# One Conformer-RWKV block on one core: PSUM evacuations ahead in their queues, a copy from ACT to POOL, an output product begun early, smaller modulation loads

## The chip, the cores and the metric

The program runs on one core of a Trainium2 chip, as one launch. The metric is the device time of an execution in microseconds; the kernel before was timed three times.

## The reference

One layer on 512 positions of 1024 features, in float32. The parts that the change touches, shortened:

```python
mod = silu(c) @ w_ada + b_ada            # six rows of 1024: shift1, scale1, gate1, shift2, scale2, gate2
u = modulate(rms_norm(x), shift1, scale1) @ w_in      # conv, RWKV and gate columns
y_conv = silu(layer_norm(depthwise_conv(za * sigmoid(zb), 31 taps))) @ w_conv_pw
# RWKV, 16 heads of 64: r, k, v, decay w, a, g from u and its shift by one position
S = S * w + (S @ (-kk)) * (kk * a) + v * k            # one step per position
y = S @ r
y_rwkv = ((group_norm(y) + bonus) * g) @ w_o
merged = sigmoid(g_conv) * y_conv + sigmoid(g_rwkv) * y_rwkv
x = x + gate1 * (merged @ w_out)
h2 = modulate(rms_norm(x), shift2, scale2)
return rms_norm(x + gate2 * (relu(h2 @ w_ff1) ** 2 @ w_ff2))
```

## The kernel before, in words

Features lie on partitions, the 512 positions along the row. A product with a weight matrix is made in blocks of 128 output columns. For each block `wload` (L218 to L225) brings 512 KB of weights (raw), ACT casts them to a high part wH (L223) and POOL subtracts it from them for a low part wL (L224). The block then takes 24 matmuls, for each of eight row blocks wH on the high and on the low part of the data, then wL on the high part; `wmul` issues them at L231 to L233, `block` at L528. Two raw, two wH and two wL buffers are there, three PSUM banks for sums.

The RWKV recurrence is solved in chunks of 64 positions, eight chunks, for four groups of four heads (two blocks of 128 features, b = 0 and 1). A group goes through these steps:
- keys (L691 to L694 on POOL) and `decay_k` (L700 to L707) prepare the key tile BK. Its third part is a copy of 64 partitions by 512 elements of its first part, made by ACT at L704; POOL makes k times kp at L705.
- `transposed` (L729), `gram` (L741) and `products` form the products within the chunks.
- `group_solve` inverts the triangular parts on DVE with 31 steps (L795 to L807) while TensorE has other work; `group_solve2` follows with the small products sW (L824) and sX (L831).
- `group_chain` walks the chunks. Each link is, on TensorE, L846 and L848 (ch), L859 (ch from F) and L874 (ch from UV), with the state S on DVE at L881. Between them ACT copies F (L852) and one half of UV (L862), DVE the other half (L863). In the chain of group g the keys of group g+1 are prepared as well (`between`).
- `group_post` normalizes Y on DVE (L905 to L914), then per block transposes it (post, L927), scales it with vb (L928), multiplies by g (L931) and adds (L932).

TensorE's order is pinned there. So that it has work during the solve and the chains, the blocks of w_in still to come (k, r, v, conv and gate columns) stand in a queue, and `fill(n)` issues their next n matmuls. SOLVED says how many fills stand in a solve, STAGE = 4 how many at each place in a chain. When a block ends, its sum leaves PSUM: through `shifted` (ACT L271, DVE L272) for k, r and v, through a sigmoid for a conv gate (L552) or a gate column (L947), through a product on DVE (L557) for the conv input.

The 31 convolution taps are DVE's (L155, drawn one at a time by `tap`), with five taps made by ACT into nsq (two buffers, L572) that POOL adds (L573); L575 joins them, L578 adds to csum. A scheduler orders the instructions on each engine by its own estimate of the times and by priorities; `tc.high_priority(offset=URGENT)` moves an instruction ahead, as it does F, UV and S in the chain. Each engine then runs its queue strictly in order. SP issues all the DMA.

After RWKV follow the product with w_o (the layer norm of the convolution lies inside it), with w_pw, with w_out, and the feed-forward part. The modulation rows come from w_ada: `ada_sum(m, half, pieces, alloc)` loads a half row of 2 MB in pieces and sums them on DVE (L141, L143). In the late stages a piece is 1 MB and there are three buffers (adaw); row 4's second half and row 3's first are loaded in the product with w_pw, row 3's second in that with w_out.

The functions that the change touches:

Of the kernel before, what the change touches and what calls it, by code (L numbers as in the profile page):

```python
# [28 lines left out]
SOLVED, LAST = 148, 20  # L29
# [28 lines left out]
def tile_block(ctx: ExitStack, tc: tile.TileContext, xT, vec, cst, x0, w_ada, w_in, w2a2, g2w,  # L58
# [459 lines left out]

    def pin(i):
        return tc.keep_in_program_order(i)  # L520
# [26 lines left out]
    def conv_in(p):  # L547
        sz = []

        def gate(acc):  # L550
            sz.append(t2k(tag="cv", bufs=2))
            act.activation(sz[0], acc, AF.Sigmoid)  # L552

        def times(acc):
            z = mid.tile([P, PAD + T], F32, name=nm("z"), tag="z", bufs=3)
            pool.memset(z[:, 0:PAD], 0.0)
            dve.tensor_tensor(z[:, PAD:], acc, sz[0], ALU.mult)  # L557
            set_z(p, z)

        return [((p, "b"), block(D + p * P, gate)), ((p, "z"), block(p * P, times))]  # L560
# [57 lines left out]
    def k_block(G, b):  # L618
        def done(acc):
            p = G.blocks[b]  # L620
            G.k[b] = t2k(tag="kk", bufs=2)
            shifted(acc, G.k[b], 8 + p)
            G.sq[b] = t2k()
            act.activation(G.sq[b], G.k[b], AF.Square, scale=V("k_k", p))

        return ("k", G.blocks[b]), block(R0 + D + G.blocks[b] * P, done)

    def r_block(G, b):
        def done(acc):
            G.r[b] = t2k()  # L630
            shifted(acc, G.r[b], G.blocks[b])

        return ("r", G.blocks[b]), block(R0 + G.blocks[b] * P, done)

    def v_block(G, b):
        def done(acc):
            G.v[b] = t2k()
            shifted(acc, G.v[b], 16 + G.blocks[b])

        return ("v", G.blocks[b]), block(R0 + 2 * D + G.blocks[b] * P, done)  # L640

    def low_rank(G, b):
# [17 lines left out]
        dve.tensor_tensor_scan(G.sg[b], cmask, pw, 0.0, ALU.mult, ALU.add)  # L660
# [24 lines left out]
    def keys(G, b):  # L685

        p, k, a = G.blocks[b], G.k[b], G.a[b]
        kP, kp = G.Pi[b], t2k()
        G.ap[b], G.kp[b] = kP, kp
        BK = G.BK[b] = atile("BK", (P, NCH, 3 * C), 2)  # L690
        pool.tensor_tensor(kP, k, G.Pi[b], ALU.mult)  # L691
        act.activation(kp, a, AF.Identity, scale=V("k_a", p), bias=ka1[:, p:p + 1])
        pool.tensor_tensor(BK[:, :, 0:C], r3(kP), r3(kp), ALU.mult)
        pool.tensor_tensor(kP, kP, a, ALU.mult)  # L694

    def decay_k(G, b):
        p, k, a = G.blocks[b], G.k[b], G.a[b]
        prn = pmisc(name="prn")
        for q in range(4):
            pin(pe.matmul(prn[:, q * P:(q + 1) * P], e4[:, q, :], G.rn[:, b, :], start=True, stop=True))  # L700
        ap = G.ap[b]
        BK = G.BK[b]
        dve.scalar_tensor_tensor(BK[:, :, C:2 * C], r3(ap), V("k_k", p), r3(prn), ALU.mult, ALU.mult)
        act.copy(BK[64:128, :, 2 * C:3 * C], BK[64:128, :, 0:C])  # L704
        pool.tensor_tensor(G.kp[b], k, G.kp[b], ALU.mult)  # L705
        kkn = G.kkn[b] = t2k()
        dve.scalar_tensor_tensor(kkn, k, V("k_k", p), prn, ALU.mult, ALU.mult)  # L707
# [38 lines left out]
    def values(G, b):  # L746
# [6 lines left out]
        with tc.high_priority(offset=URGENT):  # L753
# [6 lines left out]
        dve.tensor_tensor(v, pb, v, ALU.mult)  # L760
        nc.sync.dma_start(vb_d[p], v)

    def products(G):
# [4 lines left out]
        for b in range(NB):  # L768
# [3 lines left out]
            for e in range(2):  # L772
                for cq in range(2):
                    gram(G, b, e, cq)
                    tap()
                    fill(STAGE)

# [58 lines left out]
    def group_chain(G, between):  # L836
# [4 lines left out]
        for c in range(NCH):  # L841
# [9 lines left out]
            with tc.high_priority(offset=URGENT):  # L851
                act.copy(Fs, pf)  # L852
# [8 lines left out]
            with tc.high_priority(offset=URGENT):  # L861
# [3 lines left out]
            if c < NCH - 1 and S is not None:  # L865
                sp = atile("sp", (P, NB, C))
                with tc.high_priority(offset=URGENT):
                    for b in range(NB):
                        act.activation(sp[:, b], S[:, b], AF.Copy, scale=G.PC[:, b, c:c + 1])
            if c < NCH - 1:  # L870
# [5 lines left out]
                with tc.high_priority(offset=URGENT):  # L876
# [23 lines left out]
    def group_post(g, G, Y):  # L900
# [19 lines left out]
        for b in range(NB):  # L920
# [7 lines left out]
            dve.scalar_tensor_tensor(o, pt, V("gn_g", p), o, ALU.mult, ALU.add)  # L928
# [3 lines left out]
            dve.scalar_tensor_tensor(o, o, V("gn_b", p), pg, ALU.add, ALU.mult)  # L932
# [62 lines left out]
    fill(14)  # L995
# [6 lines left out]
    for g in range(4):  # L1002
# [12 lines left out]
        if g < 3:  # L1015
# [3 lines left out]
            fill(max(SOLVED - 14 - used[0], 6))  # L1019
            low_rank(Gn, 1)  # L1020
            fill(14)
        else:
            fill(SOLVED - LAST - used[0])
        fill(4)
        group_solve2(G)
        if g == 3:
# [12 lines left out]
    fill(36)  # L1039
    next(post, 0)  # L1040
    while queue:
        fill(1)
    tap(200)
# [6 lines left out]
    for j in range(KC):  # L1050
        if j < 6:
            t = t2k()
            nc.sync.dma_start(t, yo_d[j])
        else:
            t = G.vb[j - 6]
        act.copy(yH(j), t)
        dve.tensor_tensor(yL(j), t, yH(j), ALU.subtract)
    adac = lambda n: cpool.tile([P, n, 512], F32, name=nm("adac"), tag="adac", bufs=2)
    cH, cL = pair(), pair()
    ct8 = []  # L1060
    for j in range(KC):
        gt = t2k(tag="cv", bufs=2)
        nc.sync.dma_start(gt, gate_d[8 + j])
        acc = dense(w_o, 0, j * P, yH, yL)
# [44 lines left out]
    adan = lambda n: pools["B"].tile([P, n, 512], F32, name=nm("adaw"), tag="adaw", bufs=3)  # L1109
# [3 lines left out]
    for j in range(KC):  # L1113
# [6 lines left out]
        if j == 1:  # L1120
            sums.append(ada_sum(4, 1, (4, 4), adan))
# [4 lines left out]
        if j == 4:  # L1126
            sums = [ada_sum(3, 0, (4, 4), adan)]
# [5 lines left out]
    for j in range(KC):  # L1133
# [5 lines left out]
        if j == 1:  # L1139
            sums.append(ada_sum(3, 1, (4, 4), adan))  # L1140
        if j == 3:
# [45 lines left out]
    for g in range(4):  # L1187
        if g:
            rH, rL = pair(g8), pair(g8)
        for f in range(0 if g else EARLY, 8):  # L1190
            relu2(f, dense(w_ff1, 0, (g * 8 + f) * P, h2H, h2L))
            if g == 0 and f in (3, 4):
                sums = sums + [ada_sum(5, f - 3, (4, 4), adan)] if f == 4 else [ada_sum(5, 0, (4, 4), adan)]
# [114 lines left out]
```

## Time and profile before

| what | us |
|---|---|
| three runs: median (lowest to highest) | 1146.67 (1142.85 to 1154.36) |
| profiled execution | 1142.26 |
| its span | 1140.2 |

An engine is busy while an instruction of it runs. PE is TensorE, PEld its weight loads, DVE VectorE, POOL GpSimd, ACT ScalarE, SP the engine that issues DMA. The granted clock (PEclk) is a share of full speed, 2.4 GHz. In a timeline a row names its start, its length, engine, line, operation and tiles; the bracket holds the idle time of the engine just before it, and which instruction ended that. Buffer numbers are left out there. "x64" is a count of equal instructions that follow each other. Some small matmuls appear as two records, so that a set of four is x8.

### The profile page before, as it was taken

What the parts mean: (1) busy time and instruction counts of PE and PEld (TensorE: products, weight loads), DVE (VectorE), ACT (ScalarE), POOL (GpSimd) and SP (SyncE); (2) the same over time, 40 slices, a digit from 0 to 9 for tenths busy, and PEclk for the clock granted to TensorE, in tenths of its full rate; (3) what the DMA queues carried; (4) which work ended last, traced back from release to release, by engine and by line L of the source; (5) the groups of instructions that cost most, each with busy time, mean ns of one, the idle gap of its engine ahead of it and who ended that gap; (6) DMA issues with size and microseconds to landing.
All of it is one profiled execution on the core that took longest, in us unless ns stands there. A gap on an engine that the chain in (4) does not pass through costs nothing. (4 is left out here: it accounts for less than half of the span.)

```text
span 1140.2 us, 16153 instructions
## 1 busy us (share of the span) xinstructions
PE 1059.0 (93%) x6290; PEld 833.9 (73%) x6290; DVE 735.7 (65%) x1128; ACT 504.0 (44%) x856; POOL 498.7 (44%) x290
## 2 busy tenths in 40 slices
PE   6897999999879999999899988998999999999997
PEld 5775777777657766777666766886888888888886
DVE  5876587688747786698869566878513513522545
ACT  5557455655454746445443442345312413322431
POOL 4746343644271634426234343452444444444441
PEclk9999899999989998999899988999999999999998
DMA  9721232214211231117425889842333333333332
GB/s 322 220 65 51 61 116 62 84 61 133 63 47 59 63 119 34 57 51 238 138 75 175 272 288 335 282 124 72 95 92 93 94 94 107 94 93 93 102 100 75
DMA packets 188923, 136.74 MB, mean 120 GB/s; under 512 B 5424, under 2 KB 162480, under 8 KB 188848
## 3 DMA queue, kind: packets, MB, share of 16 engines
q1 hardware_dynamic: 188848, 135.73, 38.5%
q8 instruction: 49, 0.80, 0.3%
q14 instruction: 26, 0.21, 0.1%
HBM read 121.55 MB, written 14.16 MB: 119 GB/s over the span
## 5 line engine op out<-in xcount | busy, mean ns | idle before, releaser
L224 POOL TENSOR_TENSOR wL<-raw,wH 128x1024 fp32r<-128x1024 f32 x142 | 342.9, 2415 | 501.6 <-ACT wH L223 486.8
L528 PE MATMUL mm<-b,wH 128*128 128x512 f32 x832 | 283.2, 411 | 1.5 <-ACT wH L223 1.5
L223 ACT CAST wH<-raw 128x1024 fp32r<-128x1024 f32 x142 | 148.8, 1049 | 305.5 <-PE mm L232 204.5
L528 PEld LDWEIGHTS mm<-b,wH 128*128 128x128 f32 x832 | 156.9, 193 | 37.2 <-ACT wH L223 2.0
L528 PE MATMUL mm<-b,wL 128*128 128x512 f32 x416 | 171.8, 413 | 4.5 <-POOL wL L224 4.5
L155 DVE SCALAR_TENSOR_TENSOR acc<-z,vt,acc 128x512 f32<-128x512 f32 x192 | 143.6, 748 | 2.2
L232 PE MATMUL mm<-g,wH 128*128 128x512 f32 x328 | 128.2, 391 | 1.1 <-DVE g L1161 0.9
L231 PE MATMUL mm<-g,wH 128*128 128x512 f32 x328 | 128.5, 392 | 0.0
L233 PE MATMUL mm<-g,wL 128*128 128x512 f32 x328 | 127.8, 390 | 0.0
L231 PE MATMUL mm<-b,wH 128*128 128x512 f32 x304 | 121.2, 399 | 4.7 <-ACT wH L223 4.7
L233 PE MATMUL mm<-b,wL 128*128 128x512 f32 x304 | 120.6, 397 | 3.1 <-POOL wL L224 3.1
L232 PE MATMUL mm<-b,wH 128*128 128x512 f32 x304 | 120.2, 396 | 1.7 <-DVE b L1169 1.7
L1159 DVE TENSOR_TENSOR t2k<-t2k 128x512 f32<-128x512 f32 x32 | 72.7, 2278 | 57.5 <-ACT t2k L1156 57.2
L528 PEld LDWEIGHTS mm<-b,wL 128*128 128x128 f32 x416 | 80.6, 194 | 23.2 <-POOL wL L224 5.5
L1203 DVE SCALAR_TENSOR_TENSOR x<-mm,cols,x 128x512 f32<-128x512 f32 x31 | 23.3, 751 | 114.4 <-PE mm L233 114.4
L232 PEld LDWEIGHTS mm<-g,wH 128*128 128x128 f32 x328 | 61.6, 188 | 15.3 <-DVE g L1161 2.2
L231 PEld LDWEIGHTS mm<-g,wH 128*128 128x128 f32 x328 | 61.6, 188 | 14.1 <-ACT g L1160 1.2
L231 PEld LDWEIGHTS mm<-b,wH 128*128 128x128 f32 x304 | 58.4, 192 | 17.9 <-ACT wH L223 5.6
L233 PEld LDWEIGHTS mm<-g,wL 128*128 128x128 f32 x328 | 61.6, 188 | 12.9 <-issue 0.2
L233 PEld LDWEIGHTS mm<-b,wL 128*128 128x128 f32 x304 | 58.3, 192 | 16.2 <-POOL wL L224 4.3
L232 PEld LDWEIGHTS mm<-b,wH 128*128 128x128 f32 x304 | 58.4, 192 | 14.5 <-DVE b L1169 2.1
L1160 ACT CAST g<-t2k 128x512 fp32r<-128x512 f32 x32 | 19.8, 621 | 72.4 <-DVE t2k L1159 72.4
(305 smaller groups left out, 1737.7 us busy)
## 6 DMA issues: line engine op xcount, KB each, us to landing
raw<-in_w_ff_dram SPq DMA_DIRECT2D x64, 512.0 KB, 4.0
raw<-in_w_in_dram SPq DMA_DIRECT2D x54, 512.0 KB, 3.8
adaw<-in_w_ada_dram SPq DMA_DIRECT2D x10, 1024.0 KB, 7.3
gate<-cv SPq DMA_DIRECT2D x24, 256.0 KB, 3.1
adac<-in_w_ada_dram SPq DMA_DIRECT2D x24, 256.0 KB, 4.0
wa<-in_w_ada_dram SPq DMA_DIRECT2D x11, 512.0 KB, 5.4
raw<-in_w_o_dram SPq DMA_DIRECT2D x8, 512.0 KB, 4.2
t2k<-gate SPq DMA_DIRECT2D x16, 256.0 KB, 4.9
```

What stands on the lines that cost most here:

```text
L155: dve.scalar_tensor_tensor(dst if i == n - 1 else so_far, row, col, so_far, ALU.mult, ALU.add)
L223: act.copy(wH, raw)
L224: last_low[0] = pool.tensor_tensor(wL, raw, wH, ALU.subtract)
L231: steps.append(pe.matmul(acc, wH[:, kc, :], aH(kc), start=kc == 0, stop=False))
L232: steps.append(pe.matmul(acc, wH[:, kc, :], aL(kc), start=False, stop=False))
L233: steps.append(pe.matmul(acc, wL[:, kc, :], aH(kc), start=False, stop=kc == KC - 1))
L528: pin(pe.matmul(acc, a_[:, kc, :], b_(kc), start=kc == n == 0, stop=end))
L1159: dve.tensor_tensor(t, t, t, ALU.mult)
L1160: act.copy(rH(f), t)
L1203: dve.scalar_tensor_tensor(x1(j), acc, ada[:, 40 + j:41 + j], x1(j), ALU.mult, ALU.add)
```

## The change

- `lead()`: the instructions that take a finished sum out of PSUM (sigmoids, `shifted`, conv products, the decay scan of `low_rank`, the bonus product, the two operations of `group_post`) get the priority that F and UV have.
- The copy in BK is POOL's, directly after the product that it copies, in `keys`; k times kp is moved from `decay_k` to the end of a block's products (it stays on POOL).
- SOLVED is a tuple, one count per group: 138, 150, 146 and 140 instead of 148 three times and 128. `fill(22)` stands for `fill(14)` before the first `decay_k`, and `fill(STAGE)` is added after each `group_solve2`.
- After the last chain, `fill(36)` (of which the queue held 26 matmuls) goes. The first two blocks of w_o are begun on row blocks 0 to 5 (36 pinned matmuls) before the last `group_post`, and finished on row blocks 6 and 7 after it (12).
- The late modulation rows come in pieces of 0.5 MB into six buffers, and row 3 is loaded wholly in the product with w_out, at j = 0 and 2, its column made at j = 5.

Lines of the changed kernel are other numbers: L703, L704, L705 and L787 are the POOL operations L693, the new copy, L694 and L705 of before; L578, L579, L581 and L584 are L572, L573, L575 and L578; L863, L873, L880, L885, L907 are L852, L862, L869, L874, L896; L938, L940, L943 and L945 are L927, L928, L931 and L932; L1080 is the begun w_o product; L1064 is L1056.

```diff
-SOLVED, LAST = 148, 20
+SOLVED = (138, 150, 146, 140)
...
+    def lead():
+        return tc.high_priority(offset=URGENT)
...
             sz.append(t2k(tag="cv", bufs=2))
-            act.activation(sz[0], acc, AF.Sigmoid)
+            with lead():
+                act.activation(sz[0], acc, AF.Sigmoid)
...
-            shifted(acc, G.r[b], G.blocks[b])
+            with lead():
+                shifted(acc, G.r[b], G.blocks[b])
...
-        dve.tensor_tensor_scan(G.sg[b], cmask, pw, 0.0, ALU.mult, ALU.add)
+        with lead():
+            dve.tensor_tensor_scan(G.sg[b], cmask, pw, 0.0, ALU.mult, ALU.add)
...
         pool.tensor_tensor(BK[:, :, 0:C], r3(kP), r3(kp), ALU.mult)
+        pool.tensor_copy(BK[64:128, :, 2 * C:3 * C], BK[64:128, :, 0:C])
         pool.tensor_tensor(kP, kP, a, ALU.mult)
...
-        act.copy(BK[64:128, :, 2 * C:3 * C], BK[64:128, :, 0:C])
-        pool.tensor_tensor(G.kp[b], k, G.kp[b], ALU.mult)
...
                     tap()
                     fill(STAGE)
+            pool.tensor_tensor(G.kp[b], G.k[b], G.kp[b], ALU.mult)
...
-            dve.scalar_tensor_tensor(o, pt, V("gn_g", p), o, ALU.mult, ALU.add)
+            with lead():
+                dve.scalar_tensor_tensor(o, pt, V("gn_g", p), o, ALU.mult, ALU.add)
...
-            dve.scalar_tensor_tensor(o, o, V("gn_b", p), pg, ALU.add, ALU.mult)
+            with lead():
+                dve.scalar_tensor_tensor(o, o, V("gn_b", p), pg, ALU.add, ALU.mult)
...
-    fill(14)
+    fill(22)
     decay_k(G, 0)
...
-            fill(max(SOLVED - 14 - used[0], 6))
+            fill(max(SOLVED[g] - 14 - used[0], 6))
...
-            fill(SOLVED - LAST - used[0])
+            fill(SOLVED[g] - used[0])
         fill(4)
         group_solve2(G)
+        fill(STAGE)
...
     next(post)
-    fill(36)
-    next(post, 0)
     while queue:
         fill(1)
-    tap(200)
...
+    for j in range(6):
+        t = t2k()
+        nc.sync.dma_start(t, yo_d[j])
+        split_rows(j, t)
+    begun = []
+    for j in range(2):
+        wH, wL, raw = wload(w_o, 0, j * P)
+        acc = psum("mm", 3)
+
+        def some(kcs, wH=wH, wL=wL, acc=acc):
+            steps = []
+            for kc in kcs:
+                for n, (a_, b_) in enumerate(((wH, yH), (wH, yL), (wL, yH))):
+                    steps.append(pin(pe.matmul(acc, a_[:, kc, :], b_(kc), start=kc == n == 0, stop=kc == KC - 1 and n == 2)))
+            return acc, steps
+
+        some(range(6))
+        begun.append(some)
+    next(post, 0)
+    for j in (6, 7):
+        split_rows(j, G.vb[j - 6])
+    tap(200)
+
+    def out_product(j):
+        if j > 1:
+            return dense(w_o, 0, j * P, yH, yL)
+        acc, steps = begun[j]((6, 7))
...
-    adan = lambda n: pools["B"].tile([P, n, 512], F32, name=nm("adaw"), tag="adaw", bufs=3)
+    adan = lambda n: pools["B"].tile([P, n, 512], F32, name=nm("adaw"), tag="adaw", bufs=6)
...
-            sums.append(ada_sum(4, 1, (4, 4), adan))
+            sums.append(ada_sum(4, 1, (2,) * 4, adan))
...
-        if j == 4:
-            sums = [ada_sum(3, 0, (4, 4), adan)]
...
-        if j == 1:
-            sums.append(ada_sum(3, 1, (4, 4), adan))
-        if j == 3:
+        if j in (0, 2):
+            sums = ([] if j == 0 else sums) + [ada_sum(3, j // 2, (2,) * 4, adan)]
+        if j == 5:
             with after_dense():
                 ada_col(3, sums)
```

The order on POOL in the first group's chain, where the second group's keys are prepared; before:

```order
L573 TENSOR_TENSOR co_1637<-co_1637,nsq_1821 128x512
L693 TENSOR_TENSOR BK_1721<-t2k_1658,t2k_1720 128x8x64
L694 TENSOR_TENSOR t2k_1658<-t2k_1658,t2k_1302 128x512
L224 TENSOR_TENSOR wL_1745<-raw_1742,wH_1744 128x1024
L705 TENSOR_TENSOR t2k_1720<-kk_1082,t2k_1720 128x512
L693 TENSOR_TENSOR BK_1838<-t2k_1664,t2k_1837 128x8x64
L694 TENSOR_TENSOR t2k_1664<-t2k_1664,t2k_1456 128x512
L705 TENSOR_TENSOR t2k_1837<-kk_1248,t2k_1837 128x512
L573 TENSOR_TENSOR co_1637<-co_1637,nsq_1891 128x512
```

and now:

```order
L579 TENSOR_TENSOR co_1639<-co_1639,nsq_1824 128x512
L703 TENSOR_TENSOR BK_1723<-t2k_1660,t2k_1722 128x8x64
L704 COPY BK_1723<-BK_1723 64x8x64
L705 TENSOR_TENSOR t2k_1660<-t2k_1660,t2k_1310 128x512
L224 TENSOR_TENSOR wL_1746<-raw_1743,wH_1745 128x1024
L703 TENSOR_TENSOR BK_1841<-t2k_1666,t2k_1840 128x8x64
L787 TENSOR_TENSOR t2k_1722<-kk_1064,t2k_1722 128x512
L704 COPY BK_1841<-BK_1841 64x8x64
L705 TENSOR_TENSOR t2k_1666<-t2k_1666,t2k_1454 128x512
L787 TENSOR_TENSOR t2k_1840<-kk_1248,t2k_1840 128x512
L579 TENSOR_TENSOR co_1639<-co_1639,nsq_1893 128x512
```

The names are the tiles of this chain: wL_1745 and wL_1746 are the same weights, nsq_1891 and nsq_1893 the same tap. Each BK product is followed by its copy, one k-times-kp product has moved behind the wL and one before the second copy, and the same tap comes behind one copy more after the wL.

ACT writes those taps into the two nsq buffers. In the same chain, from the fourth UV copy to the fifth; before:

```order
L862 COPY UV_1223<-ch_1789 64x2x64
L223 CAST wH_1923<-raw_1921 128x1024
L704 COPY BK_1838<-BK_1838 64x8x64
L892 COPY Yt_1569<-Y_1762 128x256
L869 ACTIVATE sp_1868<-S_1808,PC_819 128x64 x2
L896 COPY Sd_630<-S_1808 64x2x64
L852 COPY F_1835<-ch_1826 128x128
L896 COPY Sd_630<-S_1808 64x2x64
L572 ACTIVATE nsq_2011<-z_455,vt 128x512
L572 ACTIVATE nsq_2206<-z_1349,vt 128x512
L862 COPY UV_1223<-ch_1857 64x2x64
```

and now, from F before the fourth:

```order
L907 COPY Sd_629<-S_1762 64x2x64 x2
L863 COPY F_1786<-ch_1777 128x128
L578 ACTIVATE nsq_2011<-z_455,vt 128x512
L578 ACTIVATE nsq_2207<-z_1349,vt 128x512
L873 COPY UV_1231<-ch_1792 64x2x64
L903 COPY Yt_1571<-Y_1765 128x256
L880 ACTIVATE sp_1870<-S_1811,PC_819 128x64 x2
L907 COPY Sd_630<-S_1811 64x2x64
L863 COPY F_1838<-ch_1829 128x128
L907 COPY Sd_630<-S_1811 64x2x64
L873 COPY UV_1231<-ch_1859 64x2x64
```

The two taps that stood between the fourth and the fifth UV copy stand ahead of the fourth; nsq_2207 takes the buffer of nsq_1893.

The order on ACT around the fourth UV copy of the second group's chain; before:

```order
L896 COPY Sd_629<-S_2924 64x2x64
L852 COPY F_2958<-ch_2949 128x128
L896 COPY Sd_629<-S_2924 64x2x64
L704 COPY BK_2896<-BK_2896 64x8x64
L704 COPY BK_3020<-BK_3020 64x8x64
L862 COPY UV_2388<-ch_2964 64x2x64
```

and now:

```order
L880 ACTIVATE sp_2994<-S_2943,PC_1657 128x64 x2
L863 COPY F_2977<-ch_2968 128x128
L907 COPY Sd_629<-S_2943 64x2x64 x2
L578 ACTIVATE nsq_3198<-z_1592,vt 128x512
L873 COPY UV_2388<-ch_2983 64x2x64
L578 ACTIVATE nsq_3239<-z_1592,vt 128x512
```

Both copies L704 are gone from the place ahead of UV; a tap into nsq stands there instead, which before came behind it.

The order on TensorE after the last chain, around the two transposes of `group_post`; before:

```order
L231 MATMUL mm_5676<-c_5571,wH_5672 128x512
L927 MATMUL post_5545<-ct,Yt_5043 128x128 x4
L931 MATMUL g_5551<-sgx,t2k_5500 128x512
L232 MATMUL mm_5676<-c_5573,wH_5672 128x512
L927 MATMUL post_5556<-ct,Yt_5043 128x128 x4
L233 MATMUL mm_5676<-c_5571,wL_5673 128x512
L231 MATMUL mm_5676<-c_5571,wH_5672 128x512
L232 MATMUL mm_5676<-c_5573,wH_5672 128x512
L233 MATMUL mm_5676<-c_5571,wL_5673 128x512
L931 MATMUL g_5562<-sgx,t2k_5502 128x512
L231 MATMUL mm_5615<-c_5572,wH_5611 128x512
```

and now:

```order
L1080 MATMUL mm_5605<-c_5549,wH_5601 128x512
L1080 MATMUL mm_5605<-c_5547,wL_5602 128x512
L938 MATMUL post_5626<-ct,Yt_5086 128x128 x4
L943 MATMUL g_5632<-sgx,t2k_5539 128x512
L938 MATMUL post_5637<-ct,Yt_5086 128x128 x4
L943 MATMUL g_5643<-sgx,t2k_5541 128x512
L1080 MATMUL mm_5580<-c_5547,wH_5576 128x512
L1080 MATMUL mm_5580<-c_5549,wH_5576 128x512
L1080 MATMUL mm_5580<-c_5547,wL_5577 128x512
```

Before, matmuls of w_o stood between the transposes and the gate products. Now the four follow each other, behind the 36 begun matmuls, and mm_5580 on the high and low parts of rows 6 and 7 comes after them.

## Rows read from the trace of the kernel before

**Rows 1.** Page, part 1: busy us (share of the span) xinstructions; PEld loads weights.

```profile
PE 1059.0 (93%) x6290; PEld 833.9 (73%) x6290; DVE 735.7 (65%) x1128; ACT 504.0 (44%) x856; POOL 498.7 (44%) x290
```

**Rows 2.** Windows: stretch, length, busy (x) by engine, PEclk, DMA share, GB/s.

```profile
329.00:339.20 10.20, 5.80 (x46) 5.47 (x47) 3.12 (x7) 4.76 (x11) 10.04 (x7) 0.50 0.27 79
547.40:554.20 6.80, 6.51 (x78) 5.06 (x80) 5.57 (x8) 2.19 (x4) 0.00 (x0) 0.51 0.01 3
697.60:707.80 10.20, 7.12 (x16) 5.19 (x17) 4.52 (x8) 2.61 (x3) 4.72 (x2) 0.51 1.06 333
```

**Rows 3.** Timeline, PE: start us, us, operation, xcount [idle before <-releaser].

```profile
115.75 0.79 PE L528 MATMUL mm<-b,wL 128*128 128x512 f32 x1 [3.11 <-POOL wL L224]
...
204.83 0.45 PE L874 MATMUL ch<-UV,bkT 128*64 128x64 f32 x8 [0.29 <-DVE UV L863]
...
207.26 0.50 PE L528 MATMUL mm<-b,wL 128*128 128x512 f32 x1 [0.42 <-POOL wL L224]
...
333.40 0.70 PE L874 MATMUL ch<-UV,bkT 128*64 128x64 f32 x8 [6.67 <-DVE UV L863]
...
405.28 0.50 PE L655 MATMUL pa<-XA,w2H 128*128 128x512 f32 x1 [2.29 <-DVE vb L932]
...
433.44 0.22 PE L831 MATMUL sX<-TT,s 32*32 32x32 f32 x2 [1.49 <-DVE t2k L660]
...
464.85 0.45 PE L874 MATMUL ch<-UV,bkT 128*64 128x64 f32 x8 [2.27 <-DVE UV L863]
...
547.69 1.92 PE L824 MATMUL sW<-s,G 32*32 32x32 f32 x64 [3.61 <-DVE s L805]
...
585.48 0.70 PE L874 MATMUL ch<-UV,bkT 128*64 128x64 f32 x8 [1.04 <-DVE UV L863]
...
609.78 0.66 PE L927 MATMUL post<-ct,Yt 128*128 128x128 f32 x4 [0.76 <-DVE Yt L914]
...
699.47 0.79 PE L231 MATMUL mm<-b,wH 128*128 128x512 f32 x1 [2.78 <-ACT wH L223]
...
701.90 0.80 PE L233 MATMUL mm<-b,wL 128*128 128x512 f32 x1 [1.22 <-POOL wL L224]
```

**Rows 4.** Chain of work that ended last, in order of time: start, us.

```profile
622.84 0.23 PE mm L231
```

**Rows 5.** Timeline, POOL: columns as in rows 3.

```profile
0.87 0.53 POOL L118 MEMSET cmask<- 128x512 f32 x1
...
113.35 2.34 POOL L224 TENSOR_TENSOR wL<-raw,wH 128x1024 fp32r<-128x1024 f32 x1
...
204.85 2.36 POOL L224 TENSOR_TENSOR wL<-raw,wH 128x1024 fp32r<-128x1024 f32 x1
...
212.23 1.29 POOL L573 TENSOR_TENSOR co<-co,nsq 128x512 f32<-128x512 f32 x1
...
328.52 2.35 POOL L224 TENSOR_TENSOR wL<-raw,wH 128x1024 fp32r<-128x1024 f32 x1
...
459.63 1.29 POOL L573 TENSOR_TENSOR co<-co,nsq 128x512 f32<-128x512 f32 x1 [2.56 <-ACT co L568]
```

**Rows 6.** Timeline, ACT, in the second and third chain.

```profile
314.50 1.28 ACT L682 ACT_TABLE_LOAD   x1
...
332.13 0.61 ACT L704 COPY BK<-BK 64x512 f32<-64x512 f32 x1 [6.83 <-POOL BK L693]
...
463.47 0.72 ACT L572 ACTIVATE nsq<-z,vt 128x512 f32<-128x512 f32 x1 [1.79 <-POOL co L573]
```

**Rows 7.** Page, part 5: group xcount | busy us, mean ns | idle before.

```profile
L155 DVE SCALAR_TENSOR_TENSOR acc<-z,vt,acc 128x512 f32<-128x512 f32 x192 | 143.6, 748 | 2.2
```

**Rows 8.** Timeline, DVE, after the last chain.

```profile
597.50 1.22 DVE L905 TENSOR_REDUCE st<-Yt 128x16 f32<-128x1024 f32 x1 [1.32 <-ACT Yt L892]
...
608.50 1.22 DVE L914 TENSOR_TENSOR Yt<-Yt,st 128x1024 f32<-128x1024 f32 x1
```

**Rows 9.** Timeline, SP, its DMA queue, in the product with w_pw.

```profile
679.43 9.69 SPq L166 DMA_DIRECT2D adaw<-in_w_ada_dram  x2
```

## What the change is predicted to do

> **What bounds the kernel now.** I read four views in this order. The page: TensorE is busy 1059.0 of the 1140.2 us span [rows 1], so it is the bound, and only what happens in its 81 us of idle time can move the total. The windows by stretch: after a wait of some length TensorE's granted clock stands at 0.50 or 0.51 of full, which is the 1.2 GHz level, for some us more; 5.80, 6.51 and 7.12 us of busy time lie in three such stretches, so each of them loses 2.9 to 3.5 us beyond the wait itself [rows 2]. TensorE's timeline: the waits that end on another engine [rows 3]. Then the timelines of POOL, ACT, DVE and SP around these places, and the order of the changed kernel beside them. In a chain (L846 to L896) TensorE runs in program order and alternates short products with fills of four matmuls at 0.23 us each [rows 4]; ACT and POOL run in order too, so a wait of ACT for POOL stops the chain's copy behind it.
>
> **The sum, part by part.** All times are of the profiled execution, 1142.26 us (span and 2.06 around it); it lies 0.4% under the median of 1146.67 and 0.05% under the fastest run. TensorE's work hardly changes, so I count its waits and its clock.
>
> A copy of 64x512 on POOL shows nowhere. Below stands a memset of 128x512 at 0.53, above a two-input operation at 1.29 [rows 5]. I take 0.9, the middle, since it reads one operand where the one has none and the other two. The Trainium skill ("GPSIMD Engine Reference", section "Engine selection") says that one-input operations run near line rate there and two-input ones at about half of VectorE's speed. No row here shows the copy; by that rule it would be near the memset's 0.53 (an estimate), and the sum below about 2 us smaller.
>
> *Start of the RWKV stage, +1.1 (0 to 2).* TensorE waits 3.11 at 115.75 for the wL that POOL makes from 113.35 [rows 3, 5]. The two copies go onto POOL before this wL and one L787 moves behind it: 1.8 less 1.25 later, 0.55; the first transposes, 0.6 of work that stood in this gap, now come behind it. The 8 added fills hide an earlier small wait, but only bring TensorE to this wL sooner.
>
> *First solve, +0.3 (0 to 2).* Ten fills fewer, 2.3, against 8 more before it; VectorE's own stalls there shrink too.
>
> *First chain, +6.6, and +3 for the clock.* Here the change costs. Before, POOL's wL (204.85 + 2.36) came with a wait of only 0.42 at 207.26 [rows 3, 5], since its first reader stood behind a link of the chain. By the order the new weight block begins two fills sooner, so its first wL matmul stands ahead of the set of L874 that ran at 204.83. TensorE reaches it at about 204.0; POOL has a copy more in front and ends at 207.2 + 0.9 = 208.1: idle 4.1. Then the next UV copy on ACT stands behind an nsq (L578) that needs the buffer which POOL's L579 frees. After the wL POOL has five two-input operations (a step is 1.25, [rows 5]: 1.29 less overlap) and a copy: 208.1 + 6.25 + 0.9 = 215.25; nsq, UV and VectorE's half add 1.2: 216.5. Without that, TensorE would be at this L885 at 208.1 + 0.5 (two fills) + 0.35 (a set) + 2.0 (204.83 to 207.26 less 0.42) + 2.3 (eight fills and a set) = 213.3: idle 3.2. Together 7.3, less the 0.42 and 0.29 there were. Two new waits of this size cost the clock 0 to 3.5 each [rows 2]; I take 1.5 each.
>
> *Second chain, -3.0 (0 to -9.5).* This is the place that the moved copy is about: ACT's L704 waited 6.83 for POOL, L862 and VectorE's L863 behind it, and TensorE waited 6.67 at 333.40, then ran at half clock [rows 2, 3, 6]. With L704 gone from ACT, its queue has another waiter at the same place: nsq_3198 stands directly ahead of UV, and needs POOL's L579 for nsq_2965. Before wL_2929 POOL now has three operations fewer and a copy more (3 x 1.25 - 0.9 = 2.85), and one table load of 1.28 less on ACT ahead of its inputs [rows 6]: wL ends at 328.52 + 2.35 - 2.85 - 1.28 = 326.7. TensorE needs it in the third link's first fills, near 323, and waits some 3.6. L584 and L579 end at 329.2, nsq, UV and L874 at 330.4, against 333.40. Half clock follows these waits as it did that one.
>
> *Third group, -3.5 and +5.1.* The waits at 405.28 (2.29, for VectorE's vb) and 433.44 (1.49, for L660) go, as both operations now lead VectorE's queue: with a little left over, -3.5 (0 to -5). In its chain TensorE waited 2.27 at 464.85, since ACT's nsq waited for POOL to 463.47 [rows 3, 6]. The order keeps both nsq before this UV. POOL gets two copies (1.8) and a second wL (2.36) ahead of the L573 in question, and starts up to two table loads later (2.0); its idle 2.56 at 459.63 [rows 5] takes some: 1.8 + 2.36 + 2.0 - 2.56 = +3.6 (0 to 4.5). For the clock +1.5.
>
> *Fourth group, -6.5.* The wait of 3.61 at 547.69 meets 12 more fills (2.8) and one VectorE operation of 0.75 [rows 7] less in its solve: -3.5, and of the 3.2 for the clock 2 come back. At 585.48 the cast and the sigmoid ahead of UV are gone: -1.0.
>
> *End of RWKV, +7.0, and +2 for the clock.* VectorE's normalization runs from 597.50 to 608.50 + 1.22 = 609.7 [rows 8]. Before, 26 fills and 25 w_o matmuls (11.7 us) covered it, and the transposes waited 0.76 [rows 3]. The 26 fills are now spent earlier (8 + 16 + 2), so 36 w_o matmuls, 8.3, stand there: 0.76 + 15 x 0.23 = 4.2, and 0.6 more since ACT casts a weight ahead of the last Y copy: 4.8, or +4.0. Then post, g, post, g stand without a filler between them, and 12 w_o matmuls wait for rows 6 and 7: two L155, L940, L141, L945 on VectorE (5 x 0.66), POOL's two additions for csum that ACT now takes first, two casts. This takes about 9.3, TensorE's work in it 4.4: idle 4.9, against some 2 before: +3.0.
>
> *w_pw, -6.5 (0 to -7.5).* SP stood 9.69 at the fourth 1 MB piece, waiting for one of three buffers, with weights behind it [rows 9]; TensorE waited 2.78 and 1.22 [rows 3] and lost 3.5 to the clock. The pieces for row 3 leave this stage: 4.0 and 2.5 of the 3.5.
>
> *w_out, +1 (0 to 4).* Eight half-size pieces enter here, four of which wait for VectorE to free buffers, with weights queued behind them on SP; the worst is what w_pw had, 4.0.
>
> The half pieces elsewhere and the remaining leads cost nothing: they lie beside a TensorE that doesn't wait. Sum: 1.1 + 0.3 + 9.6 - 3.0 - 3.5 + 5.1 - 6.5 + 9.0 - 6.5 + 1 = 6.6, so 1142.3 + 6.6 = 1149: gains of 19.5 and losses of 26 that nearly cancel.
>
> **The rivals.**
> *POOL keeps up, faster.* If the first and third chain lose nothing to POOL (-14.7) and the second gets its whole 6.67 back (-3.7), the time is 1131. For it: POOL is busy under half of the span, and waited for ACT 2.56 in the third chain [rows 5]. Against it: in each chain the key products, the new copies and a weight subtraction stand in one queue, and the order puts the first reader of wL and the nsq before the copies that the chain needs.
> *The clock decides, slower.* Five places get a new or longer wait of 3 to 6 us: two in the first chain, one in the third, two at the end of RWKV. If each is followed by half clock at the 2.9 to 3.5 of [rows 2], say 3.2, they cost 16 and not the 6.5 counted, and the 4.5 of clock gains in the fourth group and w_pw are lost where a wait of 1 us remains: 1149 + 9.5 + 4.5 = 1163. It decides from three such stretches on. For it: waits of 3.61 and 4.0 had them. Against: at the end TensorE's slow work would lie beside VectorE's path.
> *The leads don't do what they say.* If VectorE has not reached the led operation sooner, because it is in a stall of its own, the 3.5 of the third group and the 1.0 of the fourth don't come, and a weight in w_pw is late for another transfer (half of the 6.5): 1149 + 7.8 = 1157.
>
> **How the numbers follow.** Forecast 0.50, POOL keeps up 0.25, clock 0.17, leads 0.08. A measurement of this kernel tells about 1% from no change. One per cent below the median is 1135, above 1158. The forecast's own range is 1140 to 1158. Faster: most of the first rival and little of the forecast, 0.25; slower: most of the second, half of the third and the forecast's upper edge, 0.23; the same: 0.52. The range reaches from the first rival's 1131 to just above the second's 1163.
>
> **What would show it.** Right: in the first chain a wait of TensorE for POOL's wL of about 4 us, and then one for UV of 3 with ACT's nsq waiting for POOL; in the second chain two waits of 3.6 and 1 where 6.67 stood; in the third a wait near 6; none above 1 at the fourth solve; post waiting 4 to 5 for VectorE and 4 to 5 us of idle up to the mean; no wait of SP over 5 in w_pw. Wrong: no wait over 1.5 in the first and third chain (then the first rival), or half clock for 6 us and more at most of the five places (the second).

## The result, and the profile after

Over 20 runs each, the changed kernel takes 1151.34 us (1142.12 to 1153.95) and the kernel before 1143.92 (1140.11 to 1154.36): a ratio of 1.0051, interval 1.0031 to 1.0071, or some 6 us slower. The profiled execution took 1153.09 with a span of 1151.3, 11.1 more than the span before.

Page, part 1, of the changed kernel (against [rows 1]):

```profile
PE 1070.2 (93%) x6290; PEld 840.9 (73%) x6290; DVE 736.3 (64%) x1128; ACT 501.6 (44%) x849; POOL 501.7 (44%) x298
```

TensorE's idle time is 1151.3 - 1070.2 = 81.1 us, and was 81.2. So the waits cancel, and all the loss is busy time. Summed over windows of 4 us, busy time times (1 - granted clock) is 41.3 us, against 28.0 before. Without it the busy time is 1028.9 and 1031.0: nearly the same work. The count is a little too high: from 130.84 to 134.85 us, at a clock of 0.50, a set of Gram products with four fills took 4.0 us, and before, at full clock, from 122.99 to 125.20, 2.2; that is 1.8 times as long and not twice.

The timeline of TensorE, with the waits that answer to those of [rows 3]:

```profile
117.32 0.80 PE L532 MATMUL mm<-b,wL 128*128 128x512 f32 x1 [6.49 <-POOL wL L224]
...
126.96 1.32 PE L750 MATMUL pG<-AR,BK 64*128 64x128 f32 x5 [3.42 <-ACT bkT L742]
...
219.43 0.80 PE L532 MATMUL mm<-b,wL 128*128 128x512 f32 x1 [4.23 <-POOL wL L224]
...
227.75 0.45 PE L885 MATMUL ch<-UV,bkT 128*64 128x64 f32 x8 [1.57 <-DVE UV L874]
...
347.97 0.50 PE L532 MATMUL mm<-b,wL 128*128 128x512 f32 x1 [3.40 <-POOL wL L224]
...
416.57 0.49 PE L664 MATMUL pa<-XA,w2H 128*128 128x512 f32 x1 [1.31 <-DVE vb L945]
...
444.82 1.92 PE L835 MATMUL sW<-s,G 32*32 32x32 f32 x64 [2.27 <-DVE s L816]
...
486.07 0.69 PE L885 MATMUL ch<-UV,bkT 128*64 128x64 f32 x8 [5.12 <-DVE UV L874]
...
567.78 1.92 PE L835 MATMUL sW<-s,G 32*32 32x32 f32 x64 [2.68 <-DVE s L816]
...
627.73 0.65 PE L938 MATMUL post<-ct,Yt 128*128 128x128 f32 x4 [3.02 <-DVE Yt L925]
...
681.26 0.50 PE L231 MATMUL mm<-b,wH 128*128 128x512 f32 x1 [1.76 <-ACT wH L223]
...
715.87 0.50 PE L233 MATMUL mm<-b,wL 128*128 128x512 f32 x1 [1.23 <-POOL wL L224]
```

Two of these waits stand where the prediction had none: the second, and the one of 2.27 in the third group's solve. The windows from 84 us to the first instruction of the first solve (columns as in [rows 2]), first of before, then of the changed kernel:

```profile
84.00:143.46 59.46, 50.70 (x253) 37.47 (x253) 37.03 (x48) 34.96 (x60) 30.59 (x25) 0.94 0.21 60
```

```profile
84.00:156.11 72.11, 60.51 (x256) 44.87 (x255) 37.82 (x49) 35.42 (x61) 34.62 (x28) 0.79 0.19 54
```

A stretch loses its idle time and busy time times (1 - clock): 8.76 + 3.0 = 11.8 us before, 11.6 + 12.7 = 24.3 now. That is +12.5 in this stretch alone, more than the whole difference. ACT and POOL show why bkT is late; first before, then the changed kernel:

```profile
117.42 0.72 ACT L572 ACTIVATE nsq<-z,vt 128x512 f32<-128x512 f32 x1 [4.47 <-POOL csum L573]
...
119.55 0.37 ACT L731 COPY bkT<-bkt 128x256 f32<-128x256 f32 x1
```

```profile
115.65 3.42 POOL L573 TENSOR_TENSOR csum<-csum,nsq 128x512 f32<-128x512 f32 x2
...
119.73 2.59 POOL L224 TENSOR_TENSOR wL<-raw,wH 128x1024 fp32r<-128x1024 f32 x1 [0.60 <-ACT wH L223]
```

```profile
120.69 0.72 ACT L578 ACTIVATE nsq<-z,vt 128x512 f32<-128x512 f32 x1 [8.33 <-POOL csum L579]
125.17 0.72 ACT L578 ACTIVATE nsq<-z,vt 128x512 f32<-128x512 f32 x1 [3.75 <-POOL csum L579]
125.79 0.35 ACT L740 COPY bkT<-bkt 128x256 f32<-128x256 f32 x1
```

```profile
108.53 0.61 POOL L704 COPY BK<-BK 64x512 f32<-64x512 f32 x1
...
114.92 2.35 POOL L224 TENSOR_TENSOR wL<-raw,wH 128x1024 fp32r<-128x1024 f32 x1
117.23 1.74 POOL L787 TENSOR_TENSOR t2k<-kk,t2k 128x512 f32<-128x512 f32 x1
118.92 1.74 POOL L579 TENSOR_TENSOR csum<-csum,nsq 128x512 f32<-128x512 f32 x1
120.62 2.85 POOL L224 TENSOR_TENSOR wL<-raw,wH 128x1024 fp32r<-128x1024 f32 x1
123.41 1.72 POOL L579 TENSOR_TENSOR csum<-csum,nsq 128x512 f32<-128x512 f32 x1
```

Two of ACT's taps now stand ahead of the copies into bkT, where before there was one. With two nsq buffers each needs a POOL addition (L579), and the second addition now comes behind a second weight subtraction; before, both additions stood ahead of it. After the wait the Gram products (L750) run at half clock for 16 us; before, they ran at full clock. A window of the changed kernel, then of before:

```profile
128.00:132.00 4.00, 4.00 (x14) 2.93 (x13) 1.35 (x2) 0.06 (x1) 0.00 (x0) 0.50 0.00 0
```

```profile
128.00:132.00 4.00, 4.00 (x25) 3.34 (x24) 1.44 (x2) 2.91 (x6) 1.83 (x1) 1.00 0.10 30
```

### The profile page after: what moved, and what is told of

Same layout as the page of the kernel before. It is cut to its first block, busy times and chain, and to the rows that moved or that the text cites. A ratio compares the mean times of both kernels' runs of the same rounds, so it can differ in the third digit from the quotient of the medians.

```text
span 1151.3 us, 16187 instructions
## 1 busy us (share of the span) xinstructions
PE 1070.2 (93%) x6290; PEld 840.9 (73%) x6290; DVE 736.3 (64%) x1128; ACT 501.6 (44%) x849; POOL 501.7 (44%) x298
## 4 chain that ended last, share of the span: by engine, by line
PE 66%; DVE 10%; POOL 4%; ACT 3%; DMA 3%; issue 2%; SPq 0%; DVEq 0%; ACTq 0%; POOLq 0%
PE mm L532 21%; PE mm L232 11%; PE mm L231 10%; PE mm L233 10%; PE pG L750 3%; DMA adac<-in_w_ada_dram 2%; POOL wL L224 1%; DVE acc L143 1%; PE Y L901 1%; DVE t2k L1197 1%; PE Y L899 1%; PE ch L885 1%; PE ch L870 1%; POOL co L579 1%; PE ch L857 1%
## 5 line engine op out<-in xcount | busy, mean ns | idle before, releaser
L532 PE MATMUL mm<-b,wH 128*128 128x512 f32 x832 | 291.9, 422 | 0.6 <-ACT wH L223 0.6
L231 PE MATMUL mm<-b,wH 128*128 128x512 f32 x304 | 119.3, 393 | 2.0 <-ACT wH L223 2.0
L232 PE MATMUL mm<-b,wH 128*128 128x512 f32 x304 | 118.7, 391 | 1.7 <-DVE b L1207 1.7
```

The lines of the kernel that those rows point to most:

```text
L231: steps.append(pe.matmul(acc, wH[:, kc, :], aH(kc), start=kc == 0, stop=False))
L232: steps.append(pe.matmul(acc, wH[:, kc, :], aL(kc), start=False, stop=False))
L532: pin(pe.matmul(acc, a_[:, kc, :], b_(kc), start=kc == n == 0, stop=end))
```

## The experiments

The theory at first: the start's loss comes from the order on POOL and ACT there; the rivals are named in the expectations. Lengths of stretches, us (start: 84 us to the first solve; a chain: from its first matmul into ch to the start of its last set of them; the fills in the chains are the same in all runs; ahead of the first `decay_k` e1, e3, e4, e8, e10, e12 and the kernel before have 14, the others 22, 1.8 us more). The first solve begins on VectorE, and TensorE has made only 2 matmuls more by then in the changed kernel than before, 126 and 124 from 84 us on. Each length is from one profiled execution; those of e2, e5 and e6 took 1141.42, 1146.52 and 1143.11 us, 7 to 9 more than the medians of their runs.

| run | start | chain 1 | chain 2 | chain 3 | chain 4 | ratio to before (interval) |
|---|---|---|---|---|---|---|
| before | 59.5 | 39.0 | 47.9 | 43.0 | 39.1 | 1 |
| changed | 72.1 | 44.6 | 42.6 | 48.4 | 37.2 | 1.0051 (1.0031 to 1.0071) |
| e1_fill14 | 69.1 | 46.9 | 47.9 | 43.5 | 39.3 | 1.0163 (1.0126 to 1.0200) |
| e2_pool_as_before | 59.2 | 44.9 | 42.1 | 47.1 | 38.7 | 0.9926 (0.9901 to 0.9952) |
| e3_fills_as_before | 70.2 | 40.0 | 49.8 | 40.8 | 40.6 | 1.0026 (1.0004 to 1.0048) |
| e4_late_only | 59.8 | 40.4 | 48.1 | 43.1 | 39.1 | 0.9956 (0.9925 to 0.9987) |
| e5_taps_behind_bkT | 64.4 | 45.1 | 43.5 | 48.4 | 37.2 | 0.9961 (0.9934 to 0.9988) |
| e6_copy_on_act | 60.5 | 44.9 | 42.1 | 47.0 | 38.7 | 0.9901 (0.9866 to 0.9936) |
| e7_no_leads | 60.4 | 42.5 | 42.5 | 46.5 | 37.2 | 0.9949 (0.9924 to 0.9975) |
| e8_leads_late | 61.2 | 38.2 | 47.6 | 40.8 | 40.5 | 0.9906 (0.9873 to 0.9939) |
| e9_all_taps_held | 61.2 | 42.7 | 42.7 | 43.0 | 38.5 | 0.9909 (0.9877 to 0.9940) |
| e10_old_fills_held | 59.6 | 37.3 | 39.5 | 37.0 | 34.6 | 0.9732 (0.9694 to 0.9770) |
| e11_new_fills_held | 60.6 | 42.6 | 42.1 | 41.2 | 38.6 | 0.9884 (0.9849 to 0.9918) |
| e12_holds_alone | 59.5 | 37.3 | 39.5 | 38.3 | 35.2 | 0.9800 (0.9774 to 0.9825) |

**The eight fills at the start (e1_fill14).**

```diff
-    fill(22)
+    fill(14)
```

> The changed kernel with fill(14) ahead of the first decay_k, as before. In the changed kernel the stretch from 84 us to the first solve took 72.1 us against 59.5: TensorE waited 6.49 for a weight block's wL, then 3.42 for ACT's copies into bkT, which stood behind two taps into nsq, and then ran 16 us at half clock. Theory A (the eight fills more cross into the next weight block, whose wL enters POOL's queue ahead of a tap, and ACT's second tap ahead of bkT): the wait for bkT falls under 0.5, the half clock behind it goes, and the first solve begins near 146: 7 to 10 us faster than the changed kernel, 1141 to 1144. Theory B (POOL's own copies and the moved products there): the wait for bkT stays over 2 and the time at 1149 to 1152. Theory C (the half clock was a chance of the one profiled execution): wait gone, but the median only 2 to 4 us lower.

1161.31 us, 10 slower than the changed kernel; none of the three theories had that time. Theory A falls: the wait for bkT is still 2.74 and 7.8 us go to half clock behind it, with one tap instead of two ahead of bkT. The start is no longer than in the changed kernel; what is lost beyond it lies in the chains (4.8 us more in sum) and behind them (545.3 us from the last chain to the end, against 537.6, with the eight fills, 1.8, made there). Eight fills fewer at the start shift where each later weight block begins; that this is the reason was not tried. ACT and TensorE in its first chain:

```profile
222.83 0.72 ACT L578 ACTIVATE nsq<-z,vt 128x512 f32<-128x512 f32 x1 [8.69 <-POOL co L579]
```

```profile
224.87 0.69 PE L870 MATMUL ch<-F,G 64*64 64x64 f32 x8 [7.97 <-ACT F L863]
```

Here a tap that waits for POOL stands ahead of F.

**POOL's part (e2_pool_as_before, e6_copy_on_act).** The first undoes the copy and the place of k times kp, the second the copy alone:

```diff
-        pool.tensor_copy(BK[64:128, :, 2 * C:3 * C], BK[64:128, :, 0:C])
...
+        act.copy(BK[64:128, :, 2 * C:3 * C], BK[64:128, :, 0:C])
         kkn = G.kkn[b] = t2k()
```

> The changed kernel with POOL's part undone: the copy in BK on ACT in decay_k, k times kp behind it. Theory A: the start stays slow (6 for wL, a wait for bkT of 1 or more), the first and the third chain lose their new waits (44.6 and 48.4 us long, to 40 and 44), the second chain gets its 6.7 back (42.6 to 47): 3 to 5 us faster, 1146 to 1148. Theory B (POOL's copies are what the start pays for): the start goes back to 62 as well, 1136 to 1140. Rival (the copy on POOL is worth more in the chains than it costs): slower than the changed kernel, 1153 or more.

> The changed kernel with the copy in BK on ACT again, k times kp left at the end of the products. By the order of the instructions POOL then has both weight subtractions ahead of both taps at the start, as in the run with POOL's part undone, and ACT one tap less ahead of bkT. Theory A (the copy is the part that costs): like that run, ratio 0.990 to 0.995, start 59 to 61. Rival (k times kp moved behind wL is what costs): start 66 or more, ratio over 0.999.

1134.67 and 1134.31 us. In both the start is back and nothing waits for bkT; so having the copy on POOL is what costs, as theory B of the first and theory A of the second had it. It is not the copy's own time: from POOL's first key product to the wL at 114.92 the changed kernel took 10.85 us, e2_pool_as_before 10.64. What differs is the order that the scheduler makes of it: with the copy on ACT both weight subtractions come ahead of both taps on POOL, and one tap fewer stands ahead of bkT on ACT. POOL in e6_copy_on_act:

```profile
114.05 5.15 POOL L224 TENSOR_TENSOR wL<-raw,wH 128x1024 fp32r<-128x1024 f32 x2
119.16 1.72 POOL L579 TENSOR_TENSOR csum<-csum,nsq 128x512 f32<-128x512 f32 x1
...
120.96 1.63 POOL L579 TENSOR_TENSOR csum<-csum,nsq 128x512 f32<-128x512 f32 x1
```

That the order is enough is shown below by e9_all_taps_held: its copies are POOL's, its taps stand behind bkT, and its start is 61.2. The chains are as in the changed kernel to 1.5 us. So neither the gain in the second chain nor most of the losses in the first and third are the copy's.

**Fills and end (e3_fills_as_before).** SOLVED, fill(14), the fills behind `group_solve2` and the end of RWKV as before.

```diff
-SOLVED = (138, 150, 146, 140)
+SOLVED, LAST = 148, 20
...
+    fill(36)
+    next(post, 0)
```

> The changed kernel with all fill counts, SOLVED and the end of RWKV as before; leads, POOL's copy and the modulation pieces stay. Theory A: the start's 10 us come back, the 4 us that the new end costs too, and the fourth solve loses about 2 again: 10 to 13 us faster than the changed kernel, 1138 to 1141, a ratio to the kernel before of 0.995 to 0.998. If the begun product pays for itself (rival): like the run with fill(14) alone or slower than it, 1142 to 1146.

1147.39 us: a miss for theory A, and 1.4 over the range of its rival. The start stays slow, so the fills are not its cause. But the chains change places: the first and third are short, and the second waits 7.41 although POOL has the copy. ACT, then TensorE, at the second chain's fourth UV:

```profile
345.38 0.72 ACT L578 ACTIVATE nsq<-z,vt 128x512 f32<-128x512 f32 x1 [5.29 <-POOL co L579]
346.13 0.26 ACT L873 COPY UV<-ch 64x128 f32<-64x128 f32 x1
```

```profile
346.76 0.70 PE L885 MATMUL ch<-UV,bkT 128*64 128x64 f32 x8 [7.41 <-DVE UV L874]
```

Where the copy waited for POOL before, a tap waits now.

**The modulation pieces (e4_late_only).** The kernel before with them alone:

```diff
-    adan = lambda n: pools["B"].tile([P, n, 512], F32, name=nm("adaw"), tag="adaw", bufs=3)
+    adan = lambda n: pools["B"].tile([P, n, 512], F32, name=nm("adaw"), tag="adaw", bufs=6)
...
-            sums.append(ada_sum(4, 1, (4, 4), adan))
+            sums.append(ada_sum(4, 1, (2,) * 4, adan))
...
```

> The kernel before with the new modulation pieces alone. By the windows of the two profiles the three products behind RWKV lost about 5 us less in the changed kernel: waits of 2.78, 1.22, 1.66 and 1.85 shrank to 1.2 at most and 3.5 of half clock at 697 went. If this is the pieces' doing: 3 to 6 us faster, 1138 to 1141, ratio 0.995 to 0.9975, no wait of TensorE over 1.5 in the product with w_pw. Rival (the waits only move to the next weights): ratio 0.999 to 1.002.

1140.25 us, as expected; one wait of 1.70 is left in the product with w_pw, over the 1.5 named (the changed kernel has one of 1.76 there, not 1.2 at most).

**Taps behind bkT (e5_taps_behind_bkT).** The direct test at the start: POOL's copies stay, ACT's taps of the first block are ordered behind the copies into bkT.

```diff
-                    act.activation(t, z[:, i // 5 + 1:i // 5 + 1 + T], AF.Copy, scale=w(i // 5 + 1))
+                    with tc.issue_after(bk_last[0]) if bk_last[0] is not None and anchor[0] is None else ExitStack():
+                        act.activation(t, z[:, i // 5 + 1:i // 5 + 1 + T], AF.Copy, scale=w(i // 5 + 1))
```

> The changed kernel with ACT's taps of the first block held behind the copies into bkT by an order hint; POOL's copies stay. Theory A (the start's loss is ACT's taps, which wait for POOL ahead of bkT, and the half clock that this wait leaves in the Gram products): no wait for bkT over 0.5, Gram products at full clock, the start 60 to 63 us against 72.1, so 9 to 12 us faster than the changed kernel, 1140 to 1143, ratio 0.995 to 0.998. Theory B (POOL's queue delays the keys and wL themselves, whatever stands on ACT): the wait for wL of 6.5 stays and half clock follows it into the Gram products; start 68 or more, 1147 to 1152.

1139.76 us: theory A, if with a start of 64.4, a little over the range named. The wait for wL is 6.51, as in the changed kernel, and half clock follows it to 124, but TensorE doesn't wait for bkT and the Gram products run at full clock:

```profile
120.00:124.00 4.00, 4.00 (x13) 3.11 (x12) 4.00 (x4) 1.11 (x3) 2.53 (x3) 0.50 0.36 106
124.00:128.00 4.00, 4.00 (x22) 2.85 (x21) 2.12 (x4) 1.83 (x4) 1.29 (x1) 0.98 0.42 123
128.00:132.00 4.00, 4.00 (x24) 3.08 (x23) 2.27 (x5) 1.64 (x2) 1.41 (x2) 1.00 0.00 0
```

**Leads (e7_no_leads, e8_leads_late).** Without POOL's part, first the leads taken away, where `lead()` becomes an empty context; then leads and pieces alone on the kernel before, with the fills of e3_fills_as_before.

```diff
-            with lead():
+            with ExitStack():
                 shifted(acc, G.k[b], 8 + p)
```

> POOL's part undone and the leads too: new fills, new end and new modulation pieces alone. Theory A (leads bring the 3.5 us of the third group and little else): 2 to 5 us slower than with POOL's part alone undone (ratio 0.9926), ratio 0.995 to 0.997, with a wait of 1 to 2.5 in the third group's solve or ahead of its decay. Rival (the leads bring nothing, or cost by the half clock at 92 us that runs with leads show and the kernel before doesn't): ratio 0.989 to 0.993 and full clock at 92.

> The kernel before with leads and modulation pieces alone (fills, end and POOL's part as before). Theory A (fills and end are worth nothing or less: the first and third chain lose 5 each, the second gains 5, the end loses or gains 2): 0.990 to 0.994, like the run with POOL's part alone undone or better. Rival (the fills shift the second chain's 6.7 away and that is worth more): ratio 0.995 to 0.999, with 6 to 7 us of wait in the second chain.

1139.42 and 1135.29 us. The leads' own worth is not settled: 0.9949 without, 0.9926 with, in intervals that overlap, and so do those of e4_late_only (0.9956) and e8_leads_late (0.9906), which has the leads beside the pieces. Leads and pieces alone do as well as all parts but POOL's, so fills and end bring nothing there that shows. The second chain keeps its wait of 6.63 in e8_leads_late, as its rival had it.

**All of ACT's waits for POOL out of the chain (e9 to e12).** Each tap is held behind the newest copy into UV (at the start into bkT), and where ACT makes the copy in BK, that too. e9_all_taps_held is the changed kernel so; e10_old_fills_held the kernel of e8_leads_late; e11_new_fills_held that of e6_copy_on_act; e12_holds_alone the kernel before.

```diff
-                    act.activation(t, z[:, i // 5 + 1:i // 5 + 1 + T], AF.Copy, scale=w(i // 5 + 1))
+                    held = uv_last[0] if uv_last[0] is not None else bk_last[0]
+                    with tc.issue_after(held) if held is not None else ExitStack():
+                        act.activation(t, z[:, i // 5 + 1:i // 5 + 1 + T], AF.Copy, scale=w(i // 5 + 1))
...
-        act.copy(BK[64:128, :, 2 * C:3 * C], BK[64:128, :, 0:C])
+        with tc.issue_after(uv_last[0]) if uv_last[0] is not None else ExitStack():
+            act.copy(BK[64:128, :, 2 * C:3 * C], BK[64:128, :, 0:C])
```

> The changed kernel with every tap of ACT held behind the newest copy into bkT or UV (in a chain one or two taps behind each UV copy, none ahead of it); POOL's copies, fills, leads and end as changed. Theory (what the changed kernel loses in its chains beyond the weight waits is ACT's tap that waits for POOL ahead of UV): the third chain loses its wait of 5.1 (48.4 us, to 43 to 44), the first its 1.6, the start stays as in the run with the taps held at the start only (64): 4 to 7 us faster than that run, ratio 0.989 to 0.993. Rival (UV waits for POOL through another instruction, or VectorE sets it): the third chain stays over 46, ratio 0.995 or more.

> Leads and modulation pieces on the kernel before, with ACT's copies in BK and its taps held behind UV or bkT. Theory: the wait of 6.6 in the second chain goes, as ACT's copy in BK no longer stands ahead of UV (47.6 us, to 41 to 42), the 2.3 in the third as well: 6 to 9 us faster than leads and pieces alone (0.9906), ratio 0.983 to 0.986. Rival (the copies, now later, are needed late by the transposes and the wait only moves behind the chain): ratio 0.988 to 0.992 with a new wait for bkT or BK after a chain.

> The changed kernel with the copy in BK on ACT, and ACT's copies and taps held behind UV or bkT. Theory: the first chain keeps its wait of 3 for a wL (45 us), since that comes with where the fills begin a weight block; the third loses 2 to 3 us; 2 to 5 us faster than the copy on ACT alone (0.9901), ratio 0.986 to 0.989, and so slower than the same holds with the fills as before.

> The kernel before with nothing but the holds: ACT's taps and copies in BK behind the newest copy into UV or bkT. Theory A (the waits that the change was after are ACT's waits for POOL ahead of UV, and an order on ACT alone removes them): the second chain from 47.9 to 40 to 42 us, the third from 43 to 38 to 40, the half clock behind them gone: ratio 0.980 to 0.987; leads and pieces then account for the rest of the 0.9732. Theory B (holds help only with the leads, since VectorE's half of UV or the sums that leave PSUM late set the chains): chains over 44 and 41, ratio 0.990 to 0.996.

1136.11, 1114.85, 1132.67 and 1119.60 us. Each theory holds in its ratio but e10's, which gains more than its range, as the first chain, the fourth and the start shrink too. In e11 the way was not the one expected: the first chain is 42.6 us with a wait of 2.14 for the wL, not 45 with 3, and the third loses 5.8, not 2 to 3. The second and third chain of e12_holds_alone, in windows:

```profile
305.78:345.26 39.48, 37.38 (x416) 28.15 (x410) 27.05 (x50) 30.47 (x68) 21.57 (x19) 1.00 0.13 41
423.38:461.70 38.32, 38.32 (x414) 29.11 (x410) 26.41 (x49) 26.55 (x64) 21.49 (x18) 0.96 0.17 50
```

The second chain idles 2.1 us at full clock, where before it idled 8.2. Idle time of the whole span is 65.8 us (81.2 before), and 19.2 go to the clock (28.0). With the holds the copy on POOL or on ACT makes no difference that shows (e9 0.9909, e11 0.9884), while the new fills and end, with k times kp in its new place, cost 1.5% (e11 0.9884, e10 0.9732). The fastest version that was run is thus the kernel before with leads, pieces and holds, 2.7% faster than it. What the hold on the taps and the hold on the copies bring there, each by itself, was not tried.

## Why the prediction was right, and where it was not

The sum gave +6.6 us for the profiled execution; the medians differ by 7.4, and the spans of the two profiled executions by 11.1. The kind of loss was right in the chains and at the end: TensorE waits for POOL's wL, ACT's taps wait for POOL ahead of UV, and half clock follows. But the sum missed its largest term, the start, and that the total came near is luck: smaller losses and larger gains elsewhere made up for part of it. Measured is how much longer a stretch became from the one profile to the other, less 0.23 us for each matmul that stands in it more than before (2 at the start, 6, 2 and 16 in the second, third and fourth group, 26 fewer at the end). A chain's stretch is that of the experiments' table:

| step | predicted | measured |
|---|---|---|
| start of RWKV | +1.1 | +12.2 |
| first solve | +0.3 | -0.2 |
| first chain | +9.6 | +5.5 |
| second group up to its chain | 0 | +2.0 |
| second chain | -3.0 | -5.3 |
| third group up to its chain | -3.5 | +0.6 |
| third chain | +5.1 | +5.5 |
| fourth group | -6.5 | -7.0 |
| end of RWKV, with w_o | +9.0 | +5.3 |
| w_pw and w_out | -5.5 | -7.3 |

- **Start: the step that failed.** The late wL was seen, and its wait of 6.49 is no more than the three waits there before together (3.11, 1.55 and 1.78). The taps were not: the prediction said that a wait of ACT for POOL stops the copy behind it, looked for such places in the chains, and not ahead of bkT. With the taps moved and nothing else (e5_taps_behind_bkT) the ratio falls from 1.0051 to 0.9961, some 10 us.
- **First chain.** Both waits came where they were forecast, 4.23 (4.1) and 1.57 (3.2), with 1.5 to the clock instead of 3. The wL wait is the fills' more than the copy's: 3.16 remain with the copy on ACT, 1.41 with the copy on POOL and the fills as before.
- **Second chain.** The wait for wL came as forecast (3.40 against 3.6); behind it neither a wait for UV nor the long half clock came. That the gain is the fills' and not the copy's is shown by e6_copy_on_act (42.1 us without POOL's copy), e3_fills_as_before (49.8 with it) and e1_fill14 (47.9 with it and all the new fills but the eight at the start).
- **Third group.** The gain of 3.5 did not come: 2.29 became 1.31, the wait of 1.49 went, and TensorE waits 2.27 for the solve's s instead, then loses 3.0 to the clock. The sum had not said what would be late next. In the chain the wait was 5.12 (6 forecast), behind a tap as forecast (the rows below): e9_all_taps_held leaves 0.69 of it. But the copies, to which 1.8 of it was put down, are not its cause: the chain takes 47.0 us without them, 40.8 with them and the fills as before.

```profile
484.70 0.72 ACT L578 ACTIVATE nsq<-z,vt 128x512 f32<-128x512 f32 x1 [1.77 <-POOL co L579]
485.44 0.26 ACT L873 COPY UV<-ch 64x128 f32<-64x128 f32 x1
```

- **Fourth group.** The size is right by luck. The wait of 3.61 shrank to 2.68 only, with 3.1 of half clock behind it as before; the rest came from smaller waits that the sum had left out (0.87, 0.96 and 1.72 between the third chain and that wait, all gone).
- **End.** 3.02 idle for post (4.8 forecast) and 0.43 + 0.19 + 0.76 after it (4.9). The clock took 4.5 between 628 and 640, not 2: TensorE's work at half clock filled much of the time that the sum had as idle, and VectorE's path from the first post to row 7 took 7.0 us (627.73 to 634.73).
- **POOL's copy** takes 0.61 us, nearer the memset's 0.53 than the 0.9 taken. The Trainium skill's rule on one-input operations ("GPSIMD Engine Reference", section "Engine selection") agrees with this row.
- **The rivals.** The clock did decide the profiled execution (13 us more at half clock), but 8 of these lie in the Gram products, none of the five places named. "POOL keeps up" is refuted: the waits in the chains came. The leads' rival stays open: e7_no_leads and e2_pool_as_before don't differ clearly.

## What to carry to other kernels

Where an engine runs its queue in order, look for every instruction that waits for a slow engine and ask what stands behind it, at all places and not only where the change is aimed. Holding side work behind the copies of the critical chain gave 2.0% alone, more than any part of the change that was run apart. Two copies of 0.61 us, moved to POOL, cost 11 us at the start (72.1 us, and 60.5 in e6_copy_on_act) through the order that the scheduler then makes.

## What the runs showed of the hardware

- Half clock that sets in behind a wait as the Gram products begin stays long: the clock stood at 0.50 from 128 to 144 us in the changed kernel, with TensorE busy all through. By busy time times (1 - clock) 8.0 us were lost there, 7.8 in e1_fill14 (124 to 140) and 6.6 in e3_fills_as_before (124 to 144), with waits of 3.42, 2.74 and 2.02 ahead of them. Elsewhere a stretch at half clock lost 1 to 5 us. What ends it was not tried.
- From 92 to 100 us the changed kernel loses 3.3 us to the clock, after a wait of 1.24 at 91 us, and the kernel before none, after one of 1.54. e12_holds_alone, whose order on ACT is that of before until 97 us, loses 3.2, e4_late_only none. e12_holds_alone has no part of the change, so the change is not needed for this loss; what decides it stays open.
